# Head products of three mixers over 64 rows, in the two row halves of the array

## The chip, the cores and the metric

The kernel runs on one core of one Trainium2 chip. A core has five engines that run side by side, each through its own instructions in order: TensorE (PE, matrix products; its weight loads are listed apart as PEld), VectorE (DVE), ScalarE (ACT), GpSimd (POOL) and SyncE (SP), which issues all DMAs of this kernel. They wait for each other by semaphores. The metric is the device time of one execution in microseconds.

## The reference

One step of a one-layer decoder on 2048 prompt tokens and 32 sample tokens (8 sequences of 4), all in f32. After an input projection, four mixers of 256 columns each run beside each other (A: gated delta rule, B: Mamba-2, C: HGRN2, D: mLSTM), each with four heads of 64 dimensions, in chunks. Then come an output projection, a layer norm and a feed-forward block. The change touches the products of keys and queries inside a chunk, over the 64 dimensions of a head:

```
# A
kk = jnp.einsum('bhrd,bhjd->bhrj', kc, kc)
m = jnp.where(strict, bc[..., :, None] * kk * decay, 0.0) + eye
qk = jnp.einsum('bhrd,bhjd->bhrj', qc, kc) * decay
# B
att = jnp.einsum('bhrd,bhjd->bhrj', qc, kc) * decay
# D
p = _masked_exp(d - m_r[..., None], incl) * jnp.einsum('bhrd,bhjd->bhrj', qc, kc)
```

## The kernel before

The large products (projections and feed-forward) run on PE as f32r products in three parts (`whi`, `wlo` and the two parts of the tokens), 512 or 272 columns at a time, into the PSUM pool `psd` (tiles `pd`). Their weights are loaded by SP into `wraw`, split by ACT (`whi`) and by POOL or DVE (`wlo`). They go through the blocks of 512 tokens: all input projections (P), then, block for block, the feed-forward part (F) with the output projection of the next block between. PE's order is this stream with the work of the mixers put in between.

What is put where is decided while the program is built. Each mixer is a Python generator that yields where it has to wait. A planner (`_Sim`, `_Run`) keeps a clock for each engine with modelled costs; after every three weight products of 512 columns (`R.tick`) it resumes the generators whose results are ready by these clocks. Everything between two yields goes out in one piece, and all engines keep the order that comes out. Two streams run beside each other: `ma` with mixer A and `mb` with B, C and D in turn, 16 prompt chunks of 128 tokens and one sample chunk of 32 each.

Mixer A (`gen_A`) loads q, k and v of a chunk (two heads a tile of 128 rows: the even head in rows 0 to 63, the odd in 64 to 127) into `laA`, and the decays into `E`. It transposes k and v on PE into a PSUM tile (`p`), from where ACT copies them to `kv`, behind four exponentials on `E` (`expE`) and one on `er`. The products of keys with keys (`pk`) and of keys with queries (`pq`) contract over 128 rows with the whole tile of two heads on one side; so that only one head counts, the other side is `kzA`, a copy of the keys in which the other head's rows are zero. It is loaded by two more DMAs. DVE multiplies `pk` with beta and `E` into `U`, then masks it to `X`, with which the triangular solve begins (over `ud32d`, `nb` and `x32`); `pq` times `E` becomes `at`.

B and D do the same with `kzD`, B for its two groups of heads (`pc`), D for four heads (`pq`); C uses `kzD` too, for other zero-padded products, written by DVE.

The mixers take their PSUM tiles from two pools with two banks each, `psa` by `pa()` for A and `psb` by `pb()` for B, C and D. A tile gets the bank of the tile before the last one and waits for its readers.

Of the kernel before, what the change touches and what calls it, by code (L numbers as in the profile page):

```python
# [10 lines left out]
F32 = mybir.dt.float32  # L11
# [9 lines left out]
D = 1024  # L21
# [420 lines left out]
def kernel(ctx: ExitStack, tc: tile.TileContext, t):  # L442
# [3 lines left out]
    cst = ctx.enter_context(tc.tile_pool(name="cst", bufs=1))  # L446
# [19 lines left out]
    mult, add, sub = ALU.mult, ALU.add, ALU.subtract  # L466
    vmax, vmin = ALU.max, ALU.min

    def dma(out, in_):
        nc.sync.dma_start(out=out, in_=in_)  # L470
        R.op("dma", R.sim.move(_ap(out), _ap(in_)))
# [13 lines left out]
    def tt(out, a, b, op, eng=None):  # L485
        (eng or V).tensor_tensor(out=out, in0=a, in1=b, op=op)
# [7 lines left out]
    def stt(out, a, s, b, op0, op1):  # L494
        V.scalar_tensor_tensor(out=out, in0=a, scalar=s, in1=b, op0=op0, op1=op1)
# [18 lines left out]
    def bc1(ap, n):  # L514
        a = ap.unsqueeze(1)
        return a.to_broadcast([ap.shape[0], n] + list(ap.shape[1:]))

    def mm(out, lhsT, rhs, start=True, stop=True):
        T.matmul(out, lhsT=lhsT, rhs=rhs, start=start, stop=stop)
# [41 lines left out]
    def tr(out, in_, k=128):  # L561
        T.transpose(out=out, in_=in_, identity=con[0:k, CCOL["ident"]:CCOL["ident"] + k])

    kzA = cst.tile([128, 4, 128], F32, name="kzA")
    kzD = cst.tile([128, 4, 128], F32, name="kzD")
    x32 = cst.tile([128, 4, 32], F32, name="x32")
    SA = cst.tile([128, 2, 2, 64], F32, name="SA")
    SB = cst.tile([128, 2, 2, 64], F32, name="SB")
    SC = cst.tile([128, 2, 2, 64], F32, name="SC")
    SD = cst.tile([128, 2, 2, 65], F32, name="SD")  # L570
    for z in (kzA, kzD, SA, SB, SC, SD):
        G.memset(z, 0.0)
    haloA = [cst.tile([128, 3], F32, name=f"haloA{i}") for i in range(6)]
    haloB = [cst.tile([128, 3], F32, name=f"haloB{i}") for i in range(4)]
# [146 lines left out]
    at = {"P": (0, 0), "F": (0, 0)}  # L721
# [583 lines left out]
    def pa():  # L1305
        return psa.tile([128, 512], F32, tag="a", name="pa_")

    def pb():
        return psb.tile([128, 512], F32, tag="b", name="pb_")
# [13 lines left out]
    def gen_A(m):  # L1323
        n = m.n
        m.t2, m.t1 = ta2, ta1
        dec = m.dec
        kz = kzA
        la = sb1.tile([128, 6, 128], F32, tag="laA", name="laA")
        dma(la[:, :, 0:n], m.U["A"][:, 0:6, :])
        for h in range(2):  # L1330
            sl = slice(64 * h, 64 * h + 64)
            dma(kz[sl, h:4:2, 0:n], m.U["A"][sl, 2:4, :])
        E = loadE(m, 0)
        er = load_rs(m, 0)
        zt = ta1(2, 128)
# [16 lines left out]
        kv = ta2(2, 4, 64)  # L1352
        cp(kv[:n].rearrange("p a h v -> p (a h v)"), p[:n])
        kT, vT = kv[:, 0], kv[:, 1]
        pk = pa()
        for h in range(4):
            mm(pk[:n, h * n:h * n + n], kz[:, h, 0:n], k_[:, h // 2, :])
        yield
        pq = pa()
        for h in range(4):  # L1360
            mm(pq[:n, h * n:h * n + n], kz[:, h, 0:n], q_[:, h // 2, :])
        U = ta2(4, 128)
        for h in range(4):
            stt(U[:n, h, 0:n], pk[:n, h * n:h * n + n], m.be[:, h:h + 1], E[:n, h, 0:n], mult, mult)
        X = ta2(4, 128)
        if dec:
            tt(X[:n, :, 0:n], U[:n, :, 0:n], bc1(C("nlm1", n, 0, n), 4), mult, tvp(4 * n))
            tt(X[:n, :, 0:n], X[:n, :, 0:n], bc1(C("ident", n, 0, n), 4), add, tvp(4 * n))
        else:
            tt(X, U, bc1(C("bd32", 128), 4), mult, tvp(512))  # L1370
        yield
        at = E
        tt(at[:n, :, 0:n], pq[:n, 0:4 * n].rearrange("p (h r) -> p h r", h=4), E[:n, :, 0:n], mult)
        yield
        if not dec:
            ud = ta1(4, 32)
# [122 lines left out]
    def gen_B(m):  # L1499
        n = m.n  # L1500
        m.t2, m.t1 = tb2, tb1
        dec = m.dec
        la = sb1.tile([128, 8, 128], F32, tag="laC", name="laC")[:, 0:4]
        dma(la[:, :, 0:n], m.U["B"][:, 0:4, :])
        for h in range(2):
            sl = slice(64 * h, 64 * h + 64)
            dma(kzD[sl, h, 0:n], m.U["B"][sl, 3, :])
        E = loadE(m, 4)
        er = load_rs(m, 4)
        zt = tb1(2, 128)  # L1510
        dma(zt[:, :, 0:n], m.U["B"][:, 4:6, :])
        yield
        if dec:
            cd = tb1(2, ND)
            f1 = []
            for p_ in range(2):
                for g in range(2):
                    f1.append(lambda p_=p_, g=g: dma_s(cd[64 * p_:64 * p_ + 64, g, :], m.U["B"][64 * g:64 * g + 64, 3, :]))
            st, f2 = load_st(t["b_ssm_in"], 64)
            yield from spaced(f1 + f2)  # L1520
        p = pb()
        for j in range(3):
            tr(p[:n, j * 128:j * 128 + 128], la[:, j, 0:n])
        maskE(m, E)
        yield
        expE(m, E, 4)
        ex(er, er)
        pc = pb()
        for g in range(2):
            mm(pc[:n, g * n:g * n + n], la[:, 2, 0:n], kzD[:, g, 0:n])  # L1530
        yield
        xd = tb1(2, 2, 64)
        dt2 = m.tsb[:, 0:4].rearrange("p (i g) -> p i g", g=2)
        tt(xd[:n], p[:n, 0:256].rearrange("p (g i v) -> p i g v", g=2, i=2), bcf(dt2, 64), mult)
        bT = tb1(128)
        cp(bT[:n], p[:n, 256:384])
        at = E
        Ev = E[:n, :, 0:n].rearrange("p (i g) r -> p i g r", g=2)
        for i in range(2):
            tt(Ev[:, i], pc[:n, 0:2 * n].rearrange("p (g r) -> p g r", g=2), Ev[:, i], mult)  # L1540
        xw = tb1(2, 2, 64)
        we2 = m.we[:, 4:8].rearrange("p (i g) -> p i g", g=2)
        tt(xw[:n], xd[:n], bcf(we2, 64), mult)
        xd4 = xd.rearrange("p i g v -> p (i g) v")
        xw4 = xw.rearrange("p i g v -> p (i g) v")
        po = pb()
        if dec:
            qd = tb1(4, ND)
            tt(qd.rearrange("p (i g) r -> p i g r", g=2), bc1(cd, 2), er.rearrange("p (i g) r -> p i g r", g=2), mult)
            qx = xpand(m, qd)  # L1550
            yield
            for k in range(4):
                for b2 in range(4):
                    mm(po[:n, k * 64:k * 64 + 64], qx[:, b2, k, :], st[b2][:, k, :], b2 == 0, False)
                mm(po[:n, k * 64:k * 64 + 64], at[:n, k, 0:n], xd4[:n, k, :], False, True)
            bv = bT[:n].rearrange("p (g c) -> p g c", g=2)
            yield from state_x(m, pb, st, t["sb_ssm"], None, lambda k: bv[:, k % 2, :], xw4, decay_x(er), 64)
        else:
            ce = tb1(2, 128)
            tt(ce, bc1(la[:, 3, :], 2), er, mult)  # L1560
            yield
            for i in range(2):
                mm(po[:, i * 128:i * 128 + 128], ce[:, i, :], SB[:, i].rearrange("p h v -> p (h v)"), True, False)
                for k in (2 * i, 2 * i + 1):
                    mm(po[:, k * 64:k * 64 + 64], at[:, k, :], xd4[:, k, :], False, k % 2 == 1)
            pS = pb()
            mm(pS[:, 0:256], bT, xw.rearrange("p i g v -> p (i g v)"))
            yield
            st_update(SB, er[:, :, 127], pS, 64)
        oT = tb1(2, 2, 64)  # L1570
        cp(oT[:n], po[:n, 0:256].rearrange("p (i g v) -> p g i v", i=2, g=2))
        yield
        pt = pb()
        for i in range(2):
            tr(pt[:, i * n:i * n + n], oT[:n, i].rearrange("p a b -> p (a b)"), n)
        yield
        w = tb1(2, 128)
        for i in range(2):
            stt(w[:, i, 0:n], la[:, i, 0:n], PR("dsk", i), pt[:, i * n:i * n + n], mult, add)
        tt(w[:, :, 0:n], w[:, :, 0:n], zt[:, :, 0:n], mult)  # L1580
        yield "pre"
        sq = tb1(2, 128)
        A(sq[:, :, 0:n], w[:, :, 0:n], AF.Square)
        yield
        pn = pb()
        if dec:
            for i in range(2):
                mm(pn[:, i * n:i * n + n], ones, sq[:, i, 0:n])
        else:
            mm(pn[:, 0:256], ones, sq.rearrange("p i r -> p (i r)"))  # L1590
        yield
        ln(sq[:, :, 0:n], pn[:, 0:2 * n].rearrange("p (i r) -> p i r", i=2), 1.0 / 128, epsT)
        ex(sq[:, :, 0:n], sq[:, :, 0:n], -0.5)
        yield
        for i in range(2):
            stt(w[:, i, 0:n], w[:, i, 0:n], PR("nB", i), sq[:, i, 0:n], mult, mult)
        m.store(2, w)
# [123 lines left out]
    def gen_D(m):  # L1721
        n = m.n
        m.t2, m.t1 = tb2, tb1
        dec = m.dec
        kz = kzD
        la = sb1.tile([128, 8, 128], F32, tag="laC", name="laC")[:, 0:6]
        dma(la[:, :, 0:n], m.U["D"][:, 0:6, :])
        for h in range(2):
            sl = slice(64 * h, 64 * h + 64)
            dma(kz[sl, h:4:2, 0:n], m.U["D"][sl, 2:4, :])  # L1730
        E = loadE(m, 8)
        er = load_rs(m, 8)
        zt = tb1(2, 128)
# [10 lines left out]
        yield  # L1744
        expE(m, E, 8)
        ex(er, er)
        pq = pb()
        for h in range(4):
            mm(pq[:n, h * n:h * n + n], kz[:, h, 0:n], la[:, h // 2, 0:n])
        yield  # L1750
        kT = tb1(4, 64)
        cp(f4(kT)[:n], p[:n, 0:256])
        va = tb1(4, 65)
        cp(va[:n, :, 0:64], p[:n, 256:512].rearrange("p (h v) -> p h v", h=4))
        G.memset(va[:n, :, 64:65], 1.0)
        at = E
        tt(at[:n, :, 0:n], pq[:n, 0:4 * n].rearrange("p (h r) -> p h r", h=4), E[:n, :, 0:n], mult)
        yield
        vw = tb1(4, 65)
        tt(vw[:n], va[:n], bcf(m.we[:, 8:12], 65), mult)  # L1760
# [513 lines left out]
```

## Time and profile before

| | us |
|---|---|
| runs (3), median | 3063.7 |
| lowest and highest run | 3060.96, 3063.87 |
| profiled execution | 3063.81 |
| its span (first to last instruction) | 3061.9 |

The page of the profile gives each engine's busy time, then groups of instructions. Nearly all instructions of this kernel are issued by one helper (line 341), so the tiles' names tell the groups apart: `pa__6645<-laA,kzA` is a product into a tile of `pa()`, from `laA` and `kzA`. An f32 product is two instructions on PE, with two weight loads. In the form `32*128 32x64` the first two numbers are rows and columns of the weights, the others rows and columns of what moves. The timeline gives start and length in us, engine, line, operation, tiles, form and count; in square brackets stands the idle time of the engine just ahead, and what ended it.

### The profile page before, as it was taken

The numbers are of one execution on the slowest core, as the hardware profiler recorded it, in microseconds if no ns is written. First come the engines' busy times: TensorE is split into PE (matmuls) and PEld (weight loads), VectorE is DVE, ScalarE is ACT, GpSimd is POOL, SyncE is SP. The second block draws the span as 40 slices with busy tenths as digits, with TensorE's granted clock in tenths as the row PEclk, the third lists the DMA queues.
The fourth block names the chain that finished last, engine by engine and source line by source line (L and its number), as shares of the span: only waits on it lengthen the run. The fifth ranks groups of instructions, "written<-read, shape, count | busy, mean of one in ns | idle before, by whom it ended". The sixth has DMA issues, their size and how long they took to land.

```text
span 3061.9 us, 48064 instructions
## 1 busy us (share of the span) xinstructions
PE 2889.6 (94%) x16668; PEld 2480.4 (81%) x16668; DVE 2141.5 (70%) x4038; ACT 1260.7 (41%) x2685; POOL 1621.9 (53%) x1993
## 2 busy tenths in 40 slices
PE   7889898999999999999999999999999999999997
PEld 7788677777777787877777778878899999878886
DVE  8677796978897687877778766767684354474445
ACT  4654565574564433333335222333542222432222
POOL 4554756585685464466443654453344444444545
PEclk9899999999999999999999999999999999999999
DMA  5775446456557444345443444444333343333333
GB/s 166 127 172 153 141 147 205 138 157 185 157 144 214 130 134 138 118 135 155 134 145 89 144 127 129 135 141 137 112 109 94 86 119 86 111 112 97 100 93 104
DMA packets 361264, 407.12 MB, mean 133 GB/s; under 512 B 65468, under 2 KB 207804, under 8 KB 361020
## 3 DMA queue, kind: packets, MB, share of 16 engines
q1 hardware_dynamic: 361020, 404.04, 46.3%
q8 instruction: 132, 2.16, 0.3%
q14 instruction: 112, 0.92, 0.1%
HBM read 340.20 MB, written 63.72 MB: 132 GB/s over the span
## 4 chain that ended last, share of the span: by engine, by line
PE 48%; DVE 20%; POOL 11%; DMA 11%; issue 6%; ACT 4%; SPq 1%; POOLq 0%; DVEq 0%; ACTq 0%
PE pd L341 40%; DVE g L341 10%; DMA nb<-ud32d 5%; POOL wlo L341 4%; DVE b L341 4%; POOL a L341 3%; POOL x L341 3%; DVE a L341 2%; ACT g L341 2%; DMA wraw<-in_w_in_u_dram 2%; DVE kzD L341 2%; SPq L470 1%; DMA wraw<-in_w_up_u_dram 1%; DMA prx<-in_a_conv_in_dram 1%; POOL g L341 1%
## 5 line engine op out<-in xcount | busy, mean ns | idle before, releaser
L341 PE MATMUL pd<-g,whi 128*128 128x512 f32 (+2 forms) x8112 | 2243.7, 361 | 21.2 <-ACT g L341 11.3
L341 POOL TENSOR_TENSOR wlo<-wraw,whi 128x512 fp32r<-128x512 f32 x769 | 1066.0, 1394 | 1236.7 <-ACT whi L341 1139.3
L341 PEld LDWEIGHTS pd<-g,whi 128*128 128x128 f32 x8112 | 1395.3, 190 | 223.5 <-ACT g L341 12.4
L341 PE MATMUL pd<-g,wlo 128*128 128x512 f32 (+2 forms) x4056 | 1310.5, 354 | 18.7 <-POOL wlo L341 18.0
L341 PEld LDWEIGHTS pd<-g,wlo 128*128 128x128 f32 x4056 | 723.3, 191 | 114.7 <-POOL wlo L341 27.0
L341 ACT ACTIVATE whi<-wraw 128x512 fp32r<-128x512 f32 x829 | 509.4, 626 | 551.0 <-PE pd L341 249.7
L341 DVE TENSOR_TENSOR g<-g 128x512 fp32r<-128x512 f32 (+5 forms) x371 | 368.7, 997 | 199.0 <-ACT g L341 190.1
L341 ACT ACTIVATE g<-pd 128x512 f32<-128x512 f32 (+1 forms) x342 | 174.1, 527 | 495.9 <-PE pd L341 494.2
L341 DVE TENSOR_TENSOR g<-g,pd 128x512 f32<-128x512 f32 (+2 forms) x288 | 159.5, 570 | 221.7 <-PE pd L341 221.0
L341 POOL TENSOR_TENSOR a<-nb,x 128x124 f32<-128x124 f32 (+30 forms) x496 | 201.7, 407 | 97.9 <-DMA nb<-ud32d 68.8
L341 ACT ACTIVATE g<-g 128x512 f32<-128x512 f32 (+5 forms) x343 | 210.0, 633 | 67.6 <-DVE g L341 60.0
L341 POOL TENSOR_TENSOR x<-x,a 128x124 f32<-128x124 f32 (+30 forms) x496 | 197.2, 398 | 38.9
L341 DVE CAST g<-g 128x512 fp32r<-128x512 f32 (+1 forms) x169 | 173.2, 1025 | 7.8 <-ACT g L341 3.0
L341 ACT ACTIVATE b<-b 128x256 f32<-128x256 f32 (+3 forms) x201 | 81.3, 405 | 166.9 <-DVE b L341 166.2
L341 DVE TENSOR_TENSOR b<-laC 128x64 f32<-128x64 f32 (+2 forms) x471 | 117.4, 307 | 9.6 <-DMA laC<-UC 9.6
L341 DVE SCALAR_TENSOR_TENSOR g<-g 128x512 f32<-128x512 f32 (+3 forms) x124 | 111.5, 905 | 17.7 <-ACT g L341 15.4
L341 DVE SCALAR_TENSOR_TENSOR g<-g,par 128x512 f32<-128x512 f32 (+1 forms) x128 | 117.5, 934 | 1.2 <-ACT g L341 1.1
L341 DVE TENSOR_TENSOR kzD<-laC,b 64x128 f32<-64x128 f32 (+1 forms) x228 | 108.4, 475 | 2.0 <-ACT b L341 0.3
L341 DVE BATCH_NORM_STATS2 bst<-g 128x6 f32<-128x512 f32 (+1 forms) x98 | 65.7, 683 | 44.4 <-ACT g L341 40.9
L341 DVE TENSOR_SCALAR g<-g 128x512 int32<-128x512 int32 (+7 forms) x137 | 72.9, 550 | 32.9 <-ACT g L341 32.1
L341 POOL TENSOR_TENSOR g<-g 128x512 f32<-128x512 f32 (+3 forms) x47 | 70.2, 1497 | 43.7 <-ACT g L341 38.9
L341 DVE TENSOR_TENSOR wlo<-wraw,whi 128x512 fp32r<-128x512 f32 x63 | 52.1, 828 | 53.4 <-ACT whi L341 53.1
(2536 smaller groups left out, 2738.0 us busy)
## 6 DMA issues: line engine op xcount, KB each, us to landing
wraw<-in_w_dn_u_dram SPq DMA_DIRECT2D x264, 256.0 KB
wraw<-in_w_up_u_dram SPq DMA_DIRECT2D x256, 256.0 KB
wraw<-in_w_in_u_dram SPq DMA_DIRECT2D x248, 256.0 KB
nb<-ud32d SPq DMA_DIRECT2D x128, 256.0 KB
wraw<-in_w_out_u_dram SPq DMA_DIRECT2D x64, 256.0 KB
UC<-g SPq DMA_DIRECT2D x40, 256.0 KB
g<-in_x_prompt_dram SPq DMA_DIRECT2D x32, 256.0 KB
hTd<-g SPq DMA_DIRECT2D x32, 256.0 KB
```

The costliest lines, as they stand in the source:

```text
L341: r = f(*a, **k)
L470: nc.sync.dma_start(out=out, in_=in_)
```

## The change

The key products use 64 rows of the array, those in which the head's dimensions lie: even heads in rows 0 to 63, odd heads in 64 to 127. The zero-padded copies for A, B and D, their DMAs and the tile `kzA` go (`kzD` stays, for C). Even and odd heads write to different PSUM banks (`pw[0]`, `pw[1]`; in B a free quarter of the transposes' bank and one more tile). In A one product now has the key on one side and query and key of the same head on the other, 256 columns, so four products take the place of eight; the yield between `pk` and `pq` goes, and `at` is formed ahead of `X`, in two instructions. In D the copies of k and v come ahead of the products, with a yield between.

```diff
-    kzA = cst.tile([128, 4, 128], F32, name="kzA")
 # gen_A
-        for h in range(2):
-            sl = slice(64 * h, 64 * h + 64)
-            dma(kz[sl, h:4:2, 0:n], m.U["A"][sl, 2:4, :])
...
         cp(kv[:n].rearrange("p a h v -> p (a h v)"), p[:n])
         kT, vT = kv[:, 0], kv[:, 1]
-        pk = pa()
-        for h in range(4):
-            mm(pk[:n, h * n:h * n + n], kz[:, h, 0:n], k_[:, h // 2, :])
-        yield
-        pq = pa()
-        for h in range(4):
-            mm(pq[:n, h * n:h * n + n], kz[:, h, 0:n], q_[:, h // 2, :])
+        pw = [pa(), pa()]
+        for i in range(2):
+            for h in range(2):
+                sl = slice(64 * h, 64 * h + 64)
+                mm(pw[h][:n, 2 * i * n:2 * i * n + 2 * n].rearrange("p (a r) -> p a r", a=2), la[sl, 2 + i, 0:n], la[sl, i:4:2, 0:n])
+        yield
         U = ta2(4, 128)
         for h in range(4):
-            stt(U[:n, h, 0:n], pk[:n, h * n:h * n + n], m.be[:, h:h + 1], E[:n, h, 0:n], mult, mult)
+            c = (h & 2) * n + n
+            stt(U[:n, h, 0:n], pw[h % 2][:n, c:c + n], m.be[:, h:h + 1], E[:n, h, 0:n], mult, mult)
+        at = E
+        for h in range(2):
+            tt(at[:n, h:4:2, 0:n], pw[h][:n, 0:4 * n].rearrange("p (i a r) -> p i a r", i=2, a=2)[:, :, 0], E[:n, h:4:2, 0:n], mult)
         X = ta2(4, 128)
...
-        yield
-        at = E
-        tt(at[:n, :, 0:n], pq[:n, 0:4 * n].rearrange("p (h r) -> p h r", h=4), E[:n, :, 0:n], mult)
         yield
 # gen_B
-        for h in range(2):
-            sl = slice(64 * h, 64 * h + 64)
-            dma(kzD[sl, h, 0:n], m.U["B"][sl, 3, :])
...
-        pc = pb()
+        pc = [p[:, 384:512], pb()]
         for g in range(2):
-            mm(pc[:n, g * n:g * n + n], la[:, 2, 0:n], kzD[:, g, 0:n])
+            sl = slice(64 * g, 64 * g + 64)
+            mm(pc[g][:n, 0:n], la[sl, 2, 0:n], la[sl, 3, 0:n])
...
-        for i in range(2):
-            tt(Ev[:, i], pc[:n, 0:2 * n].rearrange("p (g r) -> p g r", g=2), Ev[:, i], mult)
+        for g in range(2):
+            tt(Ev[:, :, g], bc1(pc[g][:n, 0:n], 2), Ev[:, :, g], mult)
 # gen_D
-        for h in range(2):
-            sl = slice(64 * h, 64 * h + 64)
-            dma(kz[sl, h:4:2, 0:n], m.U["D"][sl, 2:4, :])
...
-        pq = pb()
-        for h in range(4):
-            mm(pq[:n, h * n:h * n + n], kz[:, h, 0:n], la[:, h // 2, 0:n])
-        yield
         kT = tb1(4, 64)
         cp(f4(kT)[:n], p[:n, 0:256])
         va = tb1(4, 65)
         cp(va[:n, :, 0:64], p[:n, 256:512].rearrange("p (h v) -> p h v", h=4))
         G.memset(va[:n, :, 64:65], 1.0)
+        yield
+        pw = [pb(), pb()]
+        for i in range(2):
+            for h in range(2):
+                sl = slice(64 * h, 64 * h + 64)
+                mm(pw[h][:n, i * n:i * n + n], la[sl, 2 + i, 0:n], la[sl, i, 0:n])
+        yield
         at = E
-        tt(at[:n, :, 0:n], pq[:n, 0:4 * n].rearrange("p (h r) -> p h r", h=4), E[:n, :, 0:n], mult)
+        for h in range(2):
+            tt(at[:n, h:4:2, 0:n], pw[h][:n, 0:2 * n].rearrange("p (i r) -> p i r", i=2), E[:n, h:4:2, 0:n], mult)
```

On PE, in the eleventh chunk of mixer A, this stood before, from the transposes on (`con,laA`; `pb__15154` is a product of D, the `pd` are weight products):

```order
L341 MATMUL pa__15144<-con,laA 128x128 x3
L341 MATMUL pb__15154<-laC,kzD 128x128 [waits DMAHW1_49,PE_49]
L341 MATMUL pb__15154<-laC,kzD 128x128 [waits DMAHW2_49]
L341 MATMUL pb__15154<-laC,kzD 128x128 x2
L341 MATMUL pd<-g,whi 128x512 [waits Activation_49]
L341 MATMUL pd<-g,wlo 128x512 [waits Pool_49]
L341 MATMUL pd<-g,whi 128x512
L341 MATMUL pa__15178<-laA,kzA 128x128 [waits DMAHW1_49,DVE_49]
L341 MATMUL pa__15178<-laA,kzA 128x128 [waits DMAHW2_49]
L341 MATMUL pa__15178<-laA,kzA 128x128 x2
L341 MATMUL pd<-g,whi 128x512
L341 MATMUL pa__15192<-laA,kzA 128x128 [waits Activation_49]
```

and this stands there now (`pa__14994` is `pw[0]`, `pa__14995` is `pw[1]`):

```order
L341 MATMUL pa__14977<-con,laA 128x128 x3
L341 MATMUL pd<-g,whi 128x512
L341 MATMUL pd<-g,wlo 128x512
L341 MATMUL pd<-g,whi 128x512
L341 MATMUL pa__14994<-laA 128x256 [waits DVE_49]
L341 MATMUL pa__14995<-laA 128x256 [waits Activation_49]
L341 MATMUL pa__14994<-laA 128x256
L341 MATMUL pa__14995<-laA 128x256
```

The wait for ACT moved from the second group of four products (with three weight products between the groups, of which the first is shown) to the second of the new products. In five of the 17 chunks three weight products stand between the transposes and the new products, in the others more.

On ACT, in the same chunk, this stood before, up to the copy of the transposes:

```order
L341 ACTIVATE whi<-wraw 128x512 [waits DMAHW7_49,PE_49,Pool_49]
L341 ACTIVATE a_15082<-a_15082,tsb2p 128x128 [waits DVE_49]
L341 ACTIVATE a_15082<-a_15082,tsb2p 128x128 x3
L341 ACTIVATE a_15084<-a_15084 128x256 [waits DMAHW5_49,DMAHW4_49]
L341 ACTIVATE a_15176<-pa__15144 128x512 [waits PE_49]
```

and this stands there now:

```order
L341 ACTIVATE b_14982<-pb__14954 128x256 [waits PE_49]
L341 ACTIVATE a_14843<-a_14843,tsb2p 128x128 [waits DVE_49]
L341 ACTIVATE a_14843<-a_14843,tsb2p 128x128 x3
L341 ACTIVATE a_14845<-a_14845 128x256 [waits DMAHW1_49,DMAHW0_49]
L341 ACTIVATE a_14992<-pa__14977 128x512 [waits PE_49]
```

Behind the copy of mixer C's transposes in place of a weight split, the same five exponentials and the same copy (last row) follow each other, and it is this copy for which `pw[1]` waits.

More of the change, by code (lines that the diff above doesn't have):

```diff
@@ L570 @@
     SD = cst.tile([128, 2, 2, 65], F32, name="SD")
-    for z in (kzA, kzD, SA, SB, SC, SD):
+    for z in (kzD, SA, SB, SC, SD):
         G.memset(z, 0.0)
@@ L1326, in gen_A @@
         dec = m.dec
-        kz = kzA
         la = sb1.tile([128, 6, 128], F32, tag="laA", name="laA")
         dma(la[:, :, 0:n], m.U["A"][:, 0:6, :])
-        for h in range(2):
-            sl = slice(64 * h, 64 * h + 64)
-            dma(kz[sl, h:4:2, 0:n], m.U["A"][sl, 2:4, :])
         E = loadE(m, 0)
@@ L1724, in gen_D @@
         dec = m.dec
-        kz = kzD
         la = sb1.tile([128, 8, 128], F32, tag="laC", name="laC")[:, 0:6]
         dma(la[:, :, 0:n], m.U["D"][:, 0:6, :])
-        for h in range(2):
-            sl = slice(64 * h, 64 * h + 64)
-            dma(kz[sl, h:4:2, 0:n], m.U["D"][sl, 2:4, :])
         E = loadE(m, 8)
```

## The prediction

> **What bounds the kernel now.** I read the page first (busy shares), then busy time by stretch, then TensorE's waits, then the timeline of TensorE (PE) and ScalarE (ACT) around one chunk of mixer A.
>
> ```profile
> span 3061.9 us, 48064 instructions
> ...
> PE 2889.6 (94%) x16668; PEld 2480.4 (81%) x16668; DVE 2141.5 (70%) x4038; ACT 1260.7 (41%) x2685; POOL 1621.9 (53%) x1993
> ...
> 100.00:2280.00 2180.00, 2052.11 (x11410) 1718.30 (x11410) 1663.70 (x3386) 986.39 (x2163) 1192.75 (x1646) 0.98 0.50 143
> ...
> L341 DVE TENSOR_TENSOR kzD<-laC,b x228: 216/290/1429, 251.3 to 2240.1; 64x128 f32<-64x128 f32 x112, 64x32 f32<-64x32 f32 x2
> ```
>
> PE is busy 94% of the span, and in the stretch that holds the mixers (100 to 2280 us, the third row, in which PE's busy time stands first) it is idle 2180 - 2052.1 = 128 us, 7.5 us for each of the 17 mixer chunks (16 of 128 tokens, one of 32). So the time is PE's work plus PE's waits: what a chunk adds to either is mostly paid in full. The latency of the mixers is not paid. The last row shows mixer C's last work at 2240 us, 820 us before the end.
>
> **The products themselves.** Every f32 product stands in the trace as two instructions, so x8 is four products.
>
> ```profile
> 576.06 0.40 PE L341 MATMUL pd<-g,whi 128*128 128x512 f32 x1
> 576.30 1.05 PE L341 MATMUL pa__6645<-laA,kzA 128*128 128x128 f32 x8
> 577.11 0.48 PE L341 MATMUL pd<-g,whi 128*128 128x512 f32 x1
> 577.43 0.40 PE L341 MATMUL pd<-g,wlo 128*128 128x512 f32 x1
> ...
> 340.62 0.59 PE L341 MATMUL pb__4166<-b,con 128*128 128x256 f32 x2
> 340.87 0.58 PE L341 MATMUL pd<-g,whi 128*128 128x512 f32 x1
> 341.29 0.40 PE L341 MATMUL pd<-g,wlo 128*128 128x512 f32 x1
> ```
>
> A weight product starts every 0.23 us (576.06 to 576.30 is one step). Four key products start at 576.30 and the second weight product behind them at 577.43, so the four cost 577.43 - 0.23 - 576.30 = 0.90 us, 0.225 each. A product with 256 moving columns costs 341.29 - 0.23 - 340.62 = 0.44 us, twice as much: moved columns are paid for. The change halves A's products from eight to four and doubles their width, so their columns stay the same, and only running the two row halves side by side can save time.
>
> ```profile
> 1628.61 0.60 PE L341 MATMUL pd<-con,g 128*128 128x128 f32 x4
> 1629.14 1.10 PE L341 MATMUL pa__17820<-a,a 32*128 32x64 f32 x8
> 1630.17 0.50 PE L341 MATMUL pd<-g,whi 128*128 128x512 f32 x1
> 1630.50 0.39 PE L341 MATMUL pd<-g,wlo 128*128 128x512 f32 x1
> ```
>
> This is the nearest row to what the change makes: eight instructions that use 32 rows of the array, with 128 weight columns as before. The four transposes ahead take 0.44 us (four instructions of a kind that cost 0.90 for eight), so PE is free at 1629.05; the second weight product behind starts at 1630.50, less 0.23 is 1630.27. The group costs 1.22 us where a full-height one costs 0.90: 0.32 us for going into part of the array and back. The change adds three such excursions in each chunk (A, B, D).
>
> The Trainium skill speaks against the change here: TensorEngine Tiling (Array Packing), Key Properties under Tiling Modes, says that changing the tiling mode drains TensorE. The trace agrees, with 0.32 us an excursion; without a drain the sum below would be 3 x 0.32 x 16 = 15 us lower.
>
> Per chunk, before: A 0.90 + 0.90, D 0.90 (the same four products), B two products, 0.45; together 3.15. After, if the halves run one behind the other: A 4 x 0.44 + 0.32 = 2.08, D 0.90 + 0.32, B 0.45 + 0.32, together 4.07: +0.92, for 16 chunks **+15 us**. If they run side by side throughout: A 0.88 + 0.32, D 0.45 + 0.32, B 0.23 + 0.32, together 2.52: -0.63, **-10 us**. The trace has no two halves at work together, so both ends stand. I take the middle way: the two instructions of a product follow each other in their own half, and only the second of one runs beside the first of the next, 5 steps in place of 8 for A (5 x 0.22 + 0.32 = 1.42, -0.38); B and D, at 128 columns, load as many weights for as many columns as before, and I let them gain nothing from it (+0.32 each). Together +0.26 a chunk, **+4 us**.
>
> **The wait that the change puts into A.** The pool behind pa() has two banks. The four transposes fill one, the copy to kv on ACT empties it. Before, the key products (pk) took the other bank at once, then came a yield, then pq took the first. Now pw takes both in the same step as the copy: its second product waits for ACT (the rows of PE in the section on the change), and behind it on PE stand all weight products.
>
> ```profile
> 576.45 1.28 ACT L341 ACTIVATE a<-a,tsb0p 128x128 f32<-128x128 f32 x4 [3.27 <-DVE a L341]
> 577.64 0.40 ACT L341 ACTIVATE a<-a 128x256 f32<-128x256 f32 x1
> 577.95 0.57 ACT L341 ACTIVATE a<-pa__6613 128x512 f32<-128x512 f32 x1
> ...
> 286.01 1.05 PE L341 MATMUL pa__3606<-laA,kzA 128*128 128x128 f32 x8
> ...
> 287.92 0.57 ACT L341 ACTIVATE a<-pa__3567 128x512 f32<-128x512 f32 x1
> ...
> 1975.41 1.05 PE L341 MATMUL pa__21359<-laA,kzA 128*128 128x128 f32 x8
> ...
> 1976.19 0.57 ACT L341 ACTIVATE a<-pa__21337 128x512 f32<-128x512 f32 x1
> ...
>   ACT a L341: 9.5, 4
> ...
> PE pa__2055 L341 <- ACT a L341: 7.5, 1, 7.5
> ```
>
> The copy stands behind four exponentials and one more on ACT: 576.45 to 578.52, 2.07 us. In the first whole-speed chunk pk starts at 286.01 and the copy ends at 288.49, 2.48 us later; in the last it is 1975.41 and 1976.76, 1.35. Over the 16 chunks behind the very first the distance is 0.1 to 3.5 us, 1.64 on average. The first of the new products hides about 0.5 (0.44 and the way in). Distance less 0.5, nothing where it is shorter, sums to 19 us. PE waits ahead of A's products today for 9.5 us in 4 places, all at pq (last row but one, from the view of the tile kzA), of which 7.5 in the very first chunk (last row). That chunk waits for ACT either way and is left out; the other 2.0 go. So **+17 us**. From below: if ACT began its exponentials as the transposes end, 2.07 less the work that the new order puts between (three weight products, 0.7 us, in five chunks, 1 to 3.6 in the others) less 0.5 leaves 5.5, less 2.0 is +4. From above: +20, if the first chunk gains nothing from its missing loads. I take 17, the measured distances.
>
> **The smaller terms.** D puts a yield between its copies and pw, as A had ahead of pq, so it should wait as pq did, 2.0 us in 16: +2 (0 to 4). DVE does in A the product with E as two halves ahead of X: some 0.7 us later for the chain of A, which has 820 us of room; 0. SP loses its loads of kz:
>
> ```profile
> L470 SPq DMA_DIRECT2D kzD<-UB x32: 465/529/773, 200.2 to 2174.0; - x32
> L470 SPq DMA_DIRECT2D kzD<-UD x32: 585/598/1654, 290.2 to 2250.6; - x32
> ...
> SPq L470 <- POOL wlo L341: 938.9, 414, 9.8
> ...
> PE pd L341 <- POOL wlo L341: 18.0, 16, 2.9
> ```
>
> With as much for A's as for D's that is 32 x (0.598 + 0.529 + 0.598) = 55 us of SP's queue (medians, in ns in the rows). SP waits 939 us for buffers of the weights alone, so it is not short of time; what stands behind kz (E, laC) comes 1.2 us earlier. PE waits 18.0 us for POOL's lo halves of the weights, which late loads can explain in part; I take -3 (-8 to 0).
>
> Sum: 4 + 17 + 2 - 3 = +20 us of PE's work and waits. Part comes back: while PE waits, ACT, DVE and POOL catch up, and the 7.5 us of idleness in each chunk shrink where they are not PE's own doing. I let a third of the sum come back, -7. The profiled execution took 3063.8 us (span 3061.9 and 1.9 around it), which is the median of the runs (3063.7) but for 0.1. **Forecast 3063.8 + 13 = 3077 us**, 0.4% slower.
>
> **The rivals.**
> 1. No change. The halves run side by side (-10) while the waits come as measured (+19 - 3): +6, less a third is +4, 3068. Against it: ACT's copy stands late in nearly every chunk; for it: each part is in bounds.
> 2. Faster, by overlap of the halves. Place: the four products of A, B and D; price: -10 us, decided where A's new waits sum to less than about 4 us (9, if the loads give all of their 8). With waits of 4, D's 0 and -8 from the loads: -14, less a third is -9, 3055. The Trainium skill has the rule for this: TensorE: Matmul & The Clock Gate, The mechanism under Part 3, has weights for another row group loaded, and products of other row groups run, beside those in flight. No run here shows it yet.
> 3. Not what it says: the products are narrow in rows but there is neither a way in and out to pay nor overlap, so A costs 1.76 for 1.80 and B and D the same: 0 from products, +16 from waits and loads, less a third +11, 3075. In sign this is the forecast.
> 4. The products one behind the other, all waits paid, nothing given back: 15 + 20 + 4 = +39, 3103.
>
> **How the numbers follow.** Two runs of this kernel can be told apart from about 0.2% on, 6 us. Forecast with 3 and 4 (slower than 3070): 0.62; rival 1 (3058 to 3070): 0.20; rival 2 (faster than 3058): 0.18. The order of all engines shifts with such a change, and single waits of 3 to 8 us come and go with it, which widens each case by some 6 us. The range leaves out about 1 in 10 on each side: 3056 to 3095, from rival 2's middle to short of rival 4.
>
> **What would show it.** Right: PE's waits for ACT ahead of pw's second product sum to 15 us or more; from the start of pw to the weight product behind, A takes about 1.4 us besides its wait, D 1.2, B 0.8. Wrong: pw's second product hardly waits (then ACT's copy ran ahead of PE), or D's four products cost well under 0.8 us, which would mean that halves overlap fully and that an excursion is cheaper than in the rows of 32; or PE's other idle time falls by more than 10 us, which would be the loads or the new order.

## The result, and the profile after

The changed kernel takes **3095.5 us** (median of 4 runs) where the kernel before takes 3063.6 on the same chip: ratio 1.0099, 95% interval 1.0083 to 1.0114. It is 1.0% slower; 3077 was forecast, with a range to 3095.

The page's span and busy time of the engines, and from the view of busy time by stretches the row of the mixers (PE's busy time first; the clock, the DMA share and GB/s last):

```profile
span 3094.3 us, 47679 instructions
...
PE 2898.5 (94%) x16532; PEld 2457.3 (79%) x16532; DVE 2138.5 (69%) x4087; ACT 1255.0 (41%) x2669; POOL 1619.1 (52%) x1994
```

```profile
100.00:2280.00 2180.00, 2036.02 (x11113) 1672.39 (x11112) 1630.60 (x3357) 970.90 (x2120) 1178.44 (x1638) 0.98 0.49 140
```

In that stretch PE is idle 2180 - 2036 = 144 us, 16 more than before. The view of the tile `laA` on PE, with what ended PE's idle time ahead of products of that tile (us, times), and PE's longest waits for DVE's `a` and for the weights:

```profile
  ACT a L341: 21.4, 12
```

```profile
PE pd L341 <- POOL wlo L341: 19.0, 25, 1.4
...
PE pa__3053 L341 <- DVE a L341: 3.0, 1, 3.0
PE pa__8910 L341 <- DVE a L341: 2.9, 1, 2.9
```

The wait for ACT's copy is 21.4 us, 9.5 before, and 13.3 of it lie in the very first chunk. The timeline of PE and of ACT there:

```profile
157.10 0.70 PE L341 MATMUL pa__2066<-laA 64*128 64x256 f32 x2
171.12 0.79 PE L341 MATMUL pa__2067<-laA 64*128 64x256 f32 x1 [13.33 <-ACT a L341]
171.13 0.79 PE L341 MATMUL pa__2066<-laA 64*128 64x256 f32 x1
171.71 0.63 PE L341 MATMUL pa__2067<-laA 64*128 64x256 f32 x1
171.72 0.63 PE L341 MATMUL pa__2066<-laA 64*128 64x256 f32 x1
172.14 1.06 PE L341 MATMUL pa__2067<-laA 64*128 64x256 f32 x2
```

```profile
161.07 0.41 ACT L341 ACTIVATE g<-prx,par 128x32 f32<-128x32 f32 x1 [3.42 <-DMA prx<-in_b_conv_in_dram]
...
168.71 0.41 ACT L341 ACTIVATE g<-prx,par 128x32 f32<-128x32 f32 x1 [4.95 <-DMA prx<-in_b_conv_in_dram]
169.03 1.26 ACT L341 ACTIVATE a<-a,tsb0p 128x128 f32<-128x128 f32 x4
170.19 0.40 ACT L341 ACTIVATE a<-a 128x256 f32<-128x256 f32 x1
170.50 0.57 ACT L341 ACTIVATE a<-pa__1993 128x512 f32<-128x512 f32 x1
```

PE sends off the first product (157.10, two instructions) and then stands, with all weight products behind it, until the copy (170.50) is done; ACT itself waits twice for loads of `prx`, which the convolution behind the input projections needs. The wait also parts the pairs: the first product of the one half and the last of the other (172.14) run alone, 5 steps in place of 4.

What this does to the clock is in the busy time by stretches (PE's busy time is the second number, the granted clock the third from the end), and, with a shorter wait, in the second chunk:

```profile
164.00:168.00 4.00, 0.00 (x0) 0.00 (x0) 4.00 (x8) 0.00 (x0) 3.01 (x4) 0.50 0.82 117
168.00:172.00 4.00, 0.88 (x4) 0.79 (x5) 0.62 (x2) 2.89 (x8) 0.33 (x1) 0.50 1.13 117
172.00:176.00 4.00, 4.00 (x18) 3.25 (x17) 3.05 (x9) 0.00 (x0) 0.94 (x1) 0.56 0.46 101
...
288.00:292.00 4.00, 4.00 (x13) 3.09 (x12) 3.67 (x11) 0.83 (x3) 1.28 (x1) 0.57 0.01 2
```

```profile
287.22 0.48 PE L341 MATMUL pa__3561<-laA 64*128 64x256 f32 x1 [2.50 <-ACT a L341]
...
288.34 0.79 PE L341 MATMUL pd<-g,whi 128*128 128x512 f32 x1
288.93 0.63 PE L341 MATMUL pd<-g,wlo 128*128 128x512 f32 x1
289.36 0.63 PE L341 MATMUL pd<-g,whi 128*128 128x512 f32 x1
```

Behind a wait of 2.5 us the clock is at half for 3.4 us, and a weight product takes 0.43 us (288.93 to 289.36) where it took 0.23: the wait costs 1.7 us more than its length.

Where the 32.4 us between the two spans are, from all records of PE in the two traces (idle time is put to the instruction that waited, the rest to the one that ran; "half clock" is half of PE's busy time at a granted clock of 0.5; `px` are the transposes of `X` and of `Tm`, behind the solve; part of the half clock lies in the products of A; the wait ahead of PE's very first instruction, 13.4 and 13.8 us, is left out):

```
                                 before    after
products of A, running             28.7     29.1
  waits ahead of them               9.6     21.5   (first chunk 7.5, 13.3)
products of B and D                20.4     17.5
waits of px                         9.0     19.9
half clock                         37.6     43.2
all other waits of PE             129.1    129.2
```

The wait in A is 11.9 of the 32, px, which waits for DVE, is 10.9, the clock 5.6. Nothing came back: the other waits stayed as they were. Together the rows rise by 26 us; the other 6 lie in the running time of PE's other products.

### The profile page after: what moved, and what is told of

Same layout as the page of the kernel before. It is cut to its first block, busy times and chain, and to the rows that moved or that the text cites. A ratio compares the mean times of both kernels' runs of the same rounds, so it can differ in the third digit from the quotient of the medians.

```text
span 3094.3 us, 47679 instructions
## 1 busy us (share of the span) xinstructions
PE 2898.5 (94%) x16532; PEld 2457.3 (79%) x16532; DVE 2138.5 (69%) x4087; ACT 1255.0 (41%) x2669; POOL 1619.1 (52%) x1994
## 5 line engine op out<-in xcount | busy, mean ns | idle before, releaser
L341 PE MATMUL pd<-g,whi 128*128 128x512 f32 (+2 forms) x8112 | 2246.0, 361 | 25.2 <-DVE g L341 13.4
L341 POOL TENSOR_TENSOR wlo<-wraw,whi 128x512 fp32r<-128x512 f32 x775 | 1077.5, 1399 | 1282.4 <-ACT whi L341 1213.0
L341 DVE TENSOR_TENSOR b<-laC 128x64 f32<-128x64 f32 (+3 forms) x469 | 111.4, 296 | 0.1
L341 DVE TENSOR_SCALAR g<-g 128x512 int32<-128x512 int32 (+7 forms) x137 | 83.7, 625 | 23.3 <-ACT g L341 22.5
L341 DVE TENSOR_TENSOR b<-laC,b 128x256 f32<-128x256 f32 (+1 forms) x146 | 85.9, 588 | 3.9
```

The lines of the kernel that those rows point to most:

```text
L341: r = f(*a, **k)
```

## The experiments

Two theories stood against each other. **Theory 1**: the parts of the change cost what they cost, above all the yield that is missing ahead of `pw` in A. **Theory 2**: the yields also feed the planner, which gave all engines a new order (2760 lines of difference in PE's list of 8520), and this order costs the time.

### Parts of the change

`e1_yield_A`, the changed kernel with a yield ahead of A's products:

```diff
         kT, vT = kv[:, 0], kv[:, 1]
+        yield
         pw = [pa(), pa()]
```

> The change with one more yield in mixer A, ahead of pw, so that the planner lets other work stand between ACT's copy and the products that need its bank. Theory 1 (each part of the change has its own price: PE's idle time ahead of A's products, 21.5 us in the profile of the change against 9.6 before, comes from the missing yield): that wait falls to 10 us or less, and the time to about 3084 us. Theory 2 (the price is the new order of all engines, which the planner's settings do not fit, and any edit throws it anew): the wait ahead of A's products falls as well, but other waits change by as much in either direction, so the time may lie anywhere from 3075 to 3100.

Measured: ratio to before 1.0012 (0.9997 to 1.0027). The same line of the view of `laA`:

```profile
  ACT a L341: 5.2, 3
```

One yield takes 0.9 of the 1.0% away, and the wait with it, 21.4 to 5.2 us. That is about 3067 us beside the 3063.6 of before, less than either theory gave.

`e2_A_only` and `e3_BD_only` take the change of gen_A alone, and those of gen_B and gen_D alone:

```diff
 # gen_A, in e2_A_only alone
-        pk = pa()
...
+        pw = [pa(), pa()]
 # gen_B and gen_D, in e3_BD_only alone
-        pc = pb()
+        pc = [p[:, 384:512], pb()]
...
-        pq = pb()
+        pw = [pb(), pb()]
```

> Mixer A as changed, B and D as before. Theory 1: in the profile of the change B's excursion costs 0.62 us where its products cost 0.45 before, D's 0.85 where they cost 0.90, so undoing both is worth (0.17 - 0.05) x 16 = 2 us, and their loads come back at about nothing: 3090 to 3096 us. Theory 2: anywhere from 3075 to 3100, with PE's other waits away from A changed by more than 5 us.

> B and D as changed, mixer A as before. Theory 1: A's waits and excursions go, B and D cost 2 us together: 3064 to 3069 us. Theory 2: 3070 to 3090 us although neither B nor D waits for anything new.

Measured: A alone 1.0169 (1.0154 to 1.0185), B and D alone 1.0044 (1.0029 to 1.0059). A alone costs more than the whole, and the two together 2.1%, twice the whole: parts that are planned anew do not add up, which speaks for a share of the order. A alone, about 3115 us, lies above both ranges; B and D alone, 3077, lie in that of Theory 2.

`e4_full_height` has the changed kernel's yields, but zero-padded keys over 128 rows, in A 256 columns wide:

```diff
-                mm(pw[h][...], la[sl, 2 + i, 0:n], la[sl, i:4:2, 0:n])
+                mm(pw[h][...], kzA[:, 2 * i + h, 0:n], la[:, i:4:2, 0:n])
```

> The order, the banks and the widths of the change in A, B and D, but with zero-padded keys again, over 128 rows (the loads of kz are back). Theory 1: no way into the row halves and back (about 9 us of PE's work in the change), but no halves side by side either; A 1.76 us, D 0.90, B 0.45 a chunk, as before (3.15); A's wait stays at 10 to 20 us: about 3075 to 3085 us. Theory 2: within 3075 to 3100. If the narrow rows themselves were the cause, the time would fall back to 3064 to 3070.

Measured: 1.0193 (1.0166 to 1.022), about 3123 us and so above both ranges, 0.9% slower than with narrow rows. So narrow rows are not what costs, as far as two different orders can tell; the swaps within one order below confirm it.

### The order held fast

To hold the order, each choice of the planner was written down while one kernel was built, and read back while another was:

```diff
-            return fast or g.ready <= self.clock["pe"] + slack
+            return pick(fast or g.ready <= self.clock["pe"] + slack)
```

and so at each place where its clocks decide. All engines then keep the order of the first kernel, but for the instructions that the edit itself moves.

`o3_no_yield_order_e1` moves A's `pw` ahead of the yield (the yield stays, empty) in the order of `e1_yield_A`; `o1_whole_change_order_before` and `o2_change_with_yield_order_before` are the whole change in the order of before, without and with the yield ahead of A's `pw`; `p1_yield_order_after` moves `pw` behind the yield in the changed kernel's own order.

```diff
 # o3, against e1; p1 does the opposite to the changed kernel
-        yield
         pw = [pa(), pa()]
...
+        yield
         yield
         U = ta2(4, 128)
 # o1, A: the yields of before
             tt(X, U, bc1(C("bd32", 128), 4), mult, tvp(512, 0.0, "x"))
+        yield
         yield
 # o1 and o2, D: the yields of before
                 mm(pw[h][:n, i * n:i * n + n], la[sl, 2 + i, 0:n], la[sl, i, 0:n])
-        yield
         at = E
```

> The whole change, but every choice of the planner (which generator goes on when, which engine takes an operation) is read from a table that was written down while the kernel before was built. So the weight products, weight splits and the other mixers stand in the order of before; only A's, B's and D's own edits differ (A: both tiles of pw in the step of the copies, with no yield ahead of pw; D: copies, a yield, then pw in the step of at). Theory 1 (the prices of the edits themselves): PE waits for the copy in A as in the changed kernel or a little more, 12 to 19 us over before, products together -3 to +9 us, loads 0: ratio to before 1.003 to 1.009, 3073 to 3091 us for a before of 3063.6. Theory 2 (the new order of all engines costs the time): without the new order the ratio is under 1.003. If both share, 1.004 to 1.006, and the rest of the changed kernel's 1.0099 is the order's.

> As the run before in the same order of before, but in A pw stands one step later, behind a yield, where pq stood (U, at and X one more step later). Theory 1: the wait for the copy goes (0 to 2 us left in the 16 chunks behind the first), the narrow products cost -3 (A -0.3, B +0.17, D -0.05 us a chunk): ratio 0.998 to 1.001, and 0.4 to 0.6% under the run before, which differs in nothing but this. Theory 2 has no reason for a difference between these two, which have one order: within 0.15% of each other.

> The kernel of e1_yield_A with its own order written down and read back, but with A's pw one step earlier, in the step of the copies: on all other engines the instructions stand word for word as in e1, on PE only the four products of A move. Theory 1: the wait returns, first chunk +6 to +9, the other 16 +8 to +17 us: ratio to before 1.005 to 1.009 where e1 had 1.0012. Theory 2: 1.000 to 1.003, as e1.

> The changed kernel in its own order, written down and read back; only A's pw is put one step later, ahead of U in the step in which U stands (PE's other instructions and all other engines keep their order word for word). Theory 1 (the missing yield is the cost): PE's wait ahead of pw's second product falls from 21.5 us to 5 or less, in part into DVE, which now waits for the products a little; ratio 1.001 to 1.004 where the changed kernel had 1.0099. Theory 2 (the new order is the cost): 1.008 to 1.011. A third case: waits that are shorter also leave fewer stretches of half clock behind them; then W products lose some 5 us too and the ratio comes to 1.000 to 1.002.

Measured, with the wait for ACT ahead of A's products (us):

| order of | with the yield | without it | the wait, with and without |
|---|---|---|---|
| e1_yield_A | 1.0012 | 1.0116 (1.0095 to 1.0137) | 5.2, 35.4 |
| before | 0.9987 (0.9973 to 1.0001) | 1.0021 (1.0009 to 1.0034) | 6.8, 23.2 |
| the changed kernel | 1.0098 (1.0077 to 1.012) | 1.0099 | 16.8, 21.4 |

The line of the view of `laA` in o3:

```profile
  ACT a L362: 35.4, 13
```

In an order made for the yield its absence costs 1.04%, more than Theory 1 gave; in that of before it costs 0.34%, and there the whole change stays just under Theory 1's range. In the changed kernel's own order the outcome is Theory 2's. There the products of A gain 10.9 us by the move (6.2 of running, 4.7 of waiting), and the time stays: of the wait 14.7 us remain in the first chunk, and half clock (+6.5 us) and the waits of mixer C's products (+6.2) take up the rest. So both theories are right in part: the wait has a price, and the order that the planner makes around it has one of its own, 1.1% between the same program in the orders of before and after (0.9987 and 1.0098, D's yields apart).

`o4_change_order_of_e4` and `p2_full_height_order_after` exchange narrow and full-height products within one order; the edit is that of `e4_full_height`.

> The changed kernel itself, in the order that the planner gave e4_full_height (the same yields, zero-padded keys). Theory 1: the edits cost what they cost in the changed kernel, so its ratio, 1.008 to 1.012, comes back. Theory 2: the order decides, and the time lies by e4's, 1.015 to 1.019, less only the products' own gain in A (4 us).

> The changed kernel in its own order, but A, B and D with zero-padded keys over 128 rows again (256 columns wide in A) and their loads. This prices the narrow rows alone, with order and yields as in the changed kernel. If halves overlap and the way in and out is cheap: slower than the changed kernel, A +4, B and D +2 us of products, and the loads: ratio 1.011 to 1.014. If the 0.9% between e4_full_height and the same program with narrow rows in its order is a general price of the loads and the wider products: 1.016 to 1.021. If narrow rows cost: under 1.009.

Measured: 1.0099 (1.0076 to 1.0123) for narrow rows in the order of e4_full_height (itself 1.0193), and 1.0133 (1.0112 to 1.0153) for full height in the changed kernel's order (itself 1.0099). The first is Theory 1's value. Narrow rows with their missing loads gain 0.9 and 0.3% over full-height products of 256 columns.

`p3_A_with_yield_order_before` takes only A's narrow products, behind a yield, in the order of before; the edit is A's part of o2.

> The order of before, with A's narrow products only, behind a yield (B and D as before, with their zero-padded keys). By the traces of the run with all three narrow in this order, A gains 8.3 us on PE (work -5.5, waits -2.8) and B and D lose 7. Theory 1: 0.2 to 0.35% faster than before, ratio 0.9965 to 0.998. If the loss at B and D was only work pushed about, as 0.9987 with all three, or 0.998 to 1.000.

Measured: 0.9998 (0.9985 to 1.0011). PE's running time at A's products falls by 5.2 us, but its waits elsewhere grow by more. The hoped-for gain did not come.

### Three orders of each kernel

SLACK is the margin by which the planner goes on with a generator ahead of its data; a change of 0.01 us makes a new order and nothing else.

```diff
-SLACK = -0.25
+SLACK = -0.24
```

> The kernel before with nothing changed but the planner's SLACK (-0.26 in place of -0.25): about as many of PE's instructions change their place as by the change under study (2200 rows against 2760). It shows what a new order alone is worth. Theory 1: within 0.3% of before. Theory 2: an order moves the time by 0.5 to 1%, up or down.

> The kernel before in a third order (SLACK -0.24), so that before, the changed kernel and the one with A's yield stand in three orders each. Theory 1: 0.997 to 1.004, between the mean of the orders with the yield (0.9996) and that without (1.0093); PE's time at A's products (work and wait) 37 to 41 us as in the other two orders of before. Theory 2: spread as all others, 0.993 to 1.012.

> The changed kernel in another order (the planner's SLACK -0.24). Theory 1 (the missing yield costs about 1% in whatever order the planner makes for it): ratio to before 1.007 to 1.013. Theory 2 (the order that came out at -0.25 is an unlucky one): between 0.998 and 1.012, and the two orders of the changed kernel differ by over 0.4% from each other or from 1.0099.

> The changed kernel in a third order (SLACK -0.26). As the run before: Theory 1 1.007 to 1.013; Theory 2 anything from 0.998 to 1.012.

> The changed kernel with A's yield (e1_yield_A, 1.0012) in another order (SLACK -0.24). Theory 1: 0.998 to 1.004, below every order of the kernel without the yield. Theory 2: spread as the orders of the kernel without it, overlapping with them.

> The changed kernel with A's yield in a third order (SLACK -0.26). As the run before: Theory 1 0.998 to 1.004; Theory 2 overlapping with the orders without the yield.

Measured, ratio to before (95% intervals within 0.0023 to each side):

| kernel | -0.24 | -0.25 | -0.26 | mean |
|---|---|---|---|---|
| before | 0.9949 | 1 | 1.0028 | 0.9992 |
| changed | 1.0116 | 1.0099 | 1.0065 | 1.0093 |
| changed, with A's yield | 0.9932 | 1.0012 | 1.0045 | 0.9996 |

The same sums of PE's time as above, as means over the three orders:

```
                          before   changed   with the yield
span                      3066.1    3097.0           3067.5
A's products, running       29.0      29.4             21.8
  waits ahead of them       10.6      29.5              6.3
  (of it, first chunk)       8.2      15.2              5.1
B's and D's, running        20.1      18.5             18.4
waits of px                  8.3      15.9             12.2
half clock                  36.8      44.6             40.3
all other waits            130.4     127.6            134.6
```

Each of the planner's orders without the yield is slower than each with it or of before, if narrowly: the nearest two, 1.0065 (1.0044 to 1.0086) and 1.0045 (1.0027 to 1.0062), overlap in their intervals. Within a kernel the order is worth 0.5 to 1.1%. Of the 31 us between the means of the changed kernel and of before 19 are the wait in A, 8 the half clock, 8 the waits of px, and 4 go the other way. Theory 1 holds for the means, as far as three orders each can show; single orders go beyond its ranges (0.9949, 0.9932, and by 0.0005 1.0065 and 1.0045), as Theory 2 had it.

With the yield the change gains nothing in the mean either (0.9996 against 0.9992): A's products run 7 us less and wait 4 us less, but px, the half clock and the other waits take about 4 us more each.

The fastest kernel here is the changed one with the yield at -0.24, 0.9932 (0.9916 to 0.9949), ahead of both. But the kernel before gets 0.9949 (0.9928 to 0.997) by the same 0.01: most of that is the order's.

`s6_yield_slack_024_full_height` is that kernel in its own order, with the full-height products of e4_full_height.

> The program of s3_yield_slack_024 (0.9932) in its own order, but with zero-padded keys over 128 rows and their loads in A, B and D. It prices the narrow rows where no wait parts the pairs of products. If halves overlap as the traces show (A's products 22 us of PE, 32 at full height; B and D 18.4, 20): +10 to +15 us with the loads, ratio 0.996 to 0.999. If the narrow rows bring nothing beside the yield: 0.992 to 0.995.

Measured: 1.0006 (0.9989 to 1.0022), so narrow rows with their missing loads are worth 0.7% there, more than the 10 to 15 us that were expected. A's products run 29.8 us in place of 21.9, B's and D's 20.6 in place of 18.4; the rest has no single place in the two traces, whose spans are only 13.6 us apart.

## Why the prediction was wrong

The direction was right; the size was not.

**The step that failed** is "Part comes back: while PE waits, ACT, DVE and POOL catch up, and the 7.5 us of idleness in each chunk shrink", -7 us. In the changed kernel PE's other waits stand at 129.2 us where they stood at 129.1, and two terms that the sum did not have are added: half clock (+5.6 us; +8 in the mean of three orders) and longer waits of px (+10.9; +8).

The added half clock follows the wait in A. If each stretch is put down to PE's idle time one grid window (3.41 us) earlier, 1.5 us of it before and 7.3 after follow waits ahead of A's products (means over three orders 2.0 and 10.9); the rows at 288 us show one case. In p1, where A waits less, that share falls to 3.7 and the share of other waits grows. The waits of px do not come from the wait in A but go with the planner's order: 19.9 and 21.4 us in the changed kernel's order, with A's products in either place; 10.1 in e4's order with the same program. That `at` now stands ahead of `X` is not enough, since it does so in the order of before too, with 6.5 and 8.3 us (o1, o2). Which of the planner's choices does it was not tried, so this part of the cause stays open.

In the order of before the step did hold. There (o1, one trace) the wait in A grows by 13.7 us, the other waits fall from 129.1 to 116.4, and the whole change costs 6 us (1.0021). The prediction's terms were read from the trace of before and fit its order; that the planner orders all engines anew was given 6 us in the range, and between o1 and the changed kernel it is 24 us (1.0021 and 1.0099; o1 has the yields of before behind `X` and in D).

**The wait in A** was +17 for 16 chunks. Measured are +6 in the changed kernel (8.2 from 2.0) and +12 as the mean of its three orders: the mechanism was right, and 4 to 20 held it. In the order of before (o1) they are +13, nearer to the forecast, so it is the new order that brings the copies nearer to the products. But **the first chunk** "waits for ACT either way and is left out", and it cost 5.8 us more. ACT's timeline of the kernel before, at the same place:

```profile
161.40 0.41 ACT L341 ACTIVATE g<-prx,par 128x32 f32<-128x32 f32 x1 [2.51 <-DMA prx<-in_b_conv_in_dram]
161.72 1.26 ACT L341 ACTIVATE a<-a,tsb0p 128x128 f32<-128x128 f32 x4
162.89 0.40 ACT L341 ACTIVATE a<-a 128x256 f32<-128x256 f32 x1
163.19 0.57 ACT L341 ACTIVATE a<-pa__1964 128x512 f32<-128x512 f32 x1
```

There the exponentials follow the first of the two steps that wait for `prx`; in the new order (161.07 and 168.71 above) they follow the second, so the copy ends at 171.07 in place of 163.76. In the order of before the first chunk waits 7.7 us (o1), in the changed kernel's order 14.7 even with the products behind a yield (p1): in this kernel it is the order that sets it. (In e1's order it is the yield: 4.2 with it, 15.8 without, e1 and o3.) The order of ACT in the first chunk shows it without any run; the prediction looked at the other sixteen.

**The products** were +4: the middle way, with B and D gaining nothing from overlap. When the wait does not part them, the halves overlap completely. PE's timeline for A in e1_yield_A, and for D and B in the changed kernel, each from the last weight product ahead to the second behind:

```profile
297.01 0.40 PE L341 MATMUL pd<-g,whi 128*128 128x512 f32 x1
297.34 0.48 PE L341 MATMUL pa__3667<-laA 64*128 64x256 f32 x1
297.35 0.48 PE L341 MATMUL pa__3668<-laA 64*128 64x256 f32 x1
297.66 0.38 PE L341 MATMUL pa__3667<-laA 64*128 64x256 f32 x1
297.67 0.38 PE L341 MATMUL pa__3668<-laA 64*128 64x256 f32 x1
...
298.40 0.50 PE L341 MATMUL pd<-g,whi 128*128 128x512 f32 x1
298.74 0.39 PE L341 MATMUL pd<-g,wlo 128*128 128x512 f32 x1
```

```profile
1205.98 0.39 PE L341 MATMUL pd<-g,whi 128*128 128x512 f32 x1
1206.29 0.37 PE L341 MATMUL pb__13059<-laC 64*128 64x128 f32 x1
1206.30 0.37 PE L341 MATMUL pb__13060<-laC 64*128 64x128 f32 x1
...
1207.27 0.40 PE L341 MATMUL pd<-g,wlo 128*128 128x512 f32 x1
...
1224.53 0.40 PE L341 MATMUL pd<-g,whi 128*128 128x512 f32 x1
1224.86 0.37 PE L341 MATMUL pb__13236<-laC 64*128 64x128 f32 x1
1224.87 0.37 PE L341 MATMUL pb__13265<-laC 64*128 64x128 f32 x1
...
1225.62 0.39 PE L341 MATMUL pd<-g,wlo 128*128 128x512 f32 x1
```

The product of the odd head starts 0.01 us behind that of the even one. By the prediction's own measure (from 0.23 behind the last weight product to 0.23 ahead of the second one behind) A takes 298.74 - 0.23 - 297.24 = 1.27 us where it took 1.80, D 1207.27 - 0.23 - 1206.21 = 0.83 (0.90), B 1225.62 - 0.23 - 1224.76 = 0.63 (0.45): -0.42 a chunk, -7 us in 16, by the bound for halves "side by side throughout" and an excursion of 0.39 in place of 0.32. In the changed kernel A has none of it: it runs 29.1 us (28.7 before) since the wait parts the pairs and some of it runs at half clock; B and D run 17.5 us (20.4 before). The excursion's 0.32 was read from a row that moves 64 columns beside one that moves 128, which holds only if the weights set the pace there; that 0.39 came out so near is in part luck.

**D's wait**, +2, was 0.0. **The loads**, -3: PE's waits for POOL's lo halves stood at 18.0 and stand at 19.0 us; no gain is seen there, though all swaps in one order have the loads together with the products, so their own price was not tried. **The chain of A**, 0: the end of the mixers did not set the end, as said.

Of the signs named, the wait did come to more than 15 us (21.4), though 13.3 of it lie in the chunk that was left out; the 1.4, 1.2 and 0.8 us for A, D and B came out as 1.27, 0.83 and 0.63 where no wait parts them.

The rivals: the fourth came nearest in its sum (3103), but not by its way, since the products did not run one behind the other. The second, overlap, was right in its mechanism and was hidden by the wait; with the yield it shows at A's products, but not in the mean of the times. The third's premises, no way in and no overlap, are both false. That single waits come and go with the order was given 6 us; three orders of one kernel lie 16 to 35 us apart.

## What to carry to other kernels

An instruction that must wait costs an in-order engine its wait, what stands behind it, and here also the clock; so an edit that lets products take the last free bank has to keep the yield ahead of them. Where a planner orders a program, compare several orders of each version (a neutral number shifted a little) before a difference under 1% is put down to the edit, and hold the order fast to price one part.

## What the hardware showed

- **The clock falls after short waits.** The stretches of half clock last 3.41 us or a multiple, on a fixed grid (but for the last of each trace). Over six traces (before, after, e1, o3, s1, s3) a window of that grid at full clock in which PE was busy under 38% was followed by one at half clock 68 times in 68; at 38 to 60% 42 times in 127; above 60% 9 times in 4974. So 2.1 us of waiting are enough if they fall into one window. The Trainium skill, TensorE: Matmul & The Clock Gate, Part 1, has the halved clock after an idle window of about 3.4 us; the rows at 287 to 289 us, with a wait of 2.5 us and products on both sides of it, show it for less.
- **The two row halves work at once, weight loads too**: products of 128 and of 256 columns start 0.01 us apart in the two halves and take as long as one alone, while each excursion into 64 rows and back costs about 0.39 us (A 1.27 - 0.88, D 0.83 - 0.45, B 0.63 - 0.23). With two products of 128 columns (B) that is a loss (0.63 for 0.45), with four of 256 (A) a gain (1.27 for 1.80).
